# Gate and up projections of a decoder trunk: high and low halves of x as one 512-column operand

## The chip, the core and the metric

The kernel runs on one core of a Trainium2 chip. The metric is the device time of one execution in microseconds. Engines are called as the profile calls them: PE is TensorE's matmul, PEld its weight load, DVE is VectorE, ACT is ScalarE, POOL is GpSimd, SP is SyncE, which issues the DMAs.

## The reference

Four layers over 256 tokens of width 1024, all in float32. Each layer is a half-step SwiGLU, a token mixer and another half-step SwiGLU, each followed by a layer norm. The change touches the SwiGLU alone, which occurs eight times:

```python
D_MODEL = 1024; SEQ = 256; DEPTH = 4; D_FF = 2816

def swiglu(x, w13, w2):
    gate, up = jnp.split(x @ w13, 2, axis=-1)
    return (jax.nn.silu(gate) * up) @ w2

for i in range(DEPTH):
    x = layer_norm(ALPHA * x + 0.5 * swiglu(x, ffn1_w13[i], ffn1_w2[i]), ln_g[i, 0], ln_b[i, 0])
    ...   # token mixer: sparse attention, forgetting attention, latent attention, sparse attention
    x = layer_norm(ALPHA * x + 0.5 * swiglu(x, ffn2_w13[i], ffn2_w2[i]), ln_g[i, 2], ln_b[i, 2])
```

## The kernel before

**Three products for one.** Every float32 matrix product is made of three TensorE products in float32r. Each operand is split into a high half (the value rounded to float32r, an ACT cast) and a low half (the value minus the high half, a DVE subtraction), and high·high, high·low and low·high are added up in one PSUM bank. `mm3` and `mm3b` (lines 154 and 160) issue the three for one K tile of 128.

**Operands.** x is kept transposed: `xh` and `xl` (`new_xt`, line 191) hold its high and low halves, 8 K tiles by 256 tokens each. `transpose_x` fills them through PSUM. Weights come by `unit` (line 126): SP loads 512 KB into one of 6 `raw` buffers, ACT casts it into the first half of a `slot` (line 141), DVE subtracts into the second half (line 142). There are 15 slots, shared with other operands; a slot is given back when the products that read it are done. A product's stationary operand is 128 columns wide, its moving operand 256 or 512.

**The SwiGLU** (`ffn`, line 280) has 22 column tiles of 128 in gate and in up. In seven of the eight the first four tiles are made with x as the stationary operand (`proj`); the change leaves that. The rest goes by pairs of column tiles: 11 pairs in the first SwiGLU, 9 in the others, 74 in all. A pair has two parts, gate (part 0) and up (part 1), so there are 148 parts. A part has two units of four K tiles each, and `projb` (line 180) is called for column tile i = 0 and i = 1: for each of 8 K tiles `mm3b` issues high weight with `xh`, low weight with `xh`, high weight with `xl`, each with 256 moving columns into one half of a bank. That is 48 products in a part. The two column tiles share one bank of the tag `psa` (4 banks): `pg` for gate, `pu` for up. The attention mixer of layer 2 calls `projb` too, for 128 products of each line; the change leaves those.

After the gate part ACT takes Silu of the whole bank in one instruction (line 338; in the very first pair two, line 336); after the up part DVE multiplies by the up bank (line 341), and `split` (lines 187 and 188) makes the two halves of the result, `ht`. Behind each pair come 24 products of 512 columns of the second matmul, `out_mm` (line 256, through `mm3`, lines 156 to 158, tag `psb`), for a pair of tiles finished earlier. After the last pair `out_end` runs the tiles that are left, pair 8 first, then 9, then 10; 18 products stand ahead of the first one that reads the last pair's `ht`. A layer norm follows.

**Order.** The tile framework sets the order of each engine's instructions when the kernel is built, and each engine runs its own in that order. The order rows below name the profile's tiles with their buffer numbers.

Of the kernel before, what the change touches and what calls it, by code (L numbers as in the profile page):

```python
# [17 lines left out]
F32R = mybir.dt.float32r  # L18
AF = mybir.ActivationFunctionType
# [3 lines left out]
P = 128  # L23
D = 1024
SEQ = 256
NT = SEQ // P
DEPTH = 4
KT = D // P
# [22 lines left out]
class Net:  # L51
# [128 lines left out]
    def projb(self, us, i, out, k0=0):  # L180

        c = slice(i * P, (i + 1) * P)
        for k, (h, l) in enumerate(us, k0):
            self.mm3b(out, h[:, c], l[:, c], self.xh[:, k, :], self.xl[:, k, :], k == 0, k == KT - 1)

    def split(self, hi, lo, src):
        self.nc.scalar.copy(hi, src)  # L187
        self.nc.vector.tensor_sub(lo, src, hi.bitcast(F32))  # L188


    def new_xt(self):
        self.xh = self.t(self.sp, [P, KT, SEQ], F32R, "xh", 1)
        self.xl = self.t(self.sp, [P, KT, SEQ], F32R, "xl", 1)

    def transpose_x(self, t, h):
        ps = self.ps("b")
# [83 lines left out]
    def ffn(self, w13, w2, ln, first=False, last=False):  # L280
        nc = self.nc
        ht = {}
        self.begin_out(w2, NFF // 2, lambda i: ht[i], "b")
        f0, turns = 0, []
        if not first:

            f0 = 4
            z = self.slot(2, 4, SEQ)
            gh, gl = z[:, 0], z[:, 1]
            for i in range(4):  # L290
                ht[i] = (gh[:, i], gl[:, i])
            gate, up = self.cols(w13, 0, 512), self.cols(w13, DFF, 512)
            for t in range(NT):
                pg, pu = self.ps(), self.ps()
                self.proj(gate, t, pg)
                s = self.tok()
                nc.scalar.activation(s, pg, AF.Silu)
                if t:
                    turns.pop()()
                self.proj(up, t, pu, KT // 2)  # L300
                nc.vector.tensor_mul(s, s, pu)

                def turn(t=t, s=s):
                    pt = self.ps("b")
                    for i in range(4):
                        nc.tensor.transpose(pt[:, i * P:(i + 1) * P], s[:, i * P:(i + 1) * P], self.ident)
                    c = (slice(None), slice(None), slice(t * P, (t + 1) * P))
                    self.split(gh[c], gl[c], pt.rearrange("p (k c) -> p k c", k=4))

                turns.append(turn)  # L310
        pairs = (NFF - f0) // 2
        self.pieces = 1
        for j in range(pairs):
            f = f0 + 2 * j
            if j % 2 == 0:
                zz = self.slot(2, 2, 2, SEQ)
            cold = first and not f
            pg, pu = self.ps(), self.ps()

            p2 = self.ps()[:, SEQ:] if cold else pg[:, SEQ:]  # L320
            s = self.tok()
            for part, p in enumerate(((pg[:, :SEQ], p2), (pu[:, :SEQ], pu[:, SEQ:]))):
                c0 = part * DFF + f * P
                cut = KT // 2 if cold and not part else KT
                for k0 in range(0, KT, cut):
                    us = self.unit(self.rows(w13, k0, k0 + cut, c0, c0 + 2 * P))
                    if cut < KT and not k0:
                        self.load_x(1)
                    if k0:
                        for t in range(NT):  # L330
                            self.transpose_x(t, 1)
                    for i in range(2):
                        self.projb(us, i, p[i], k0)
                if part == 0 and cold:
                    for i in range(2):
                        nc.scalar.activation(s[:, i * SEQ:(i + 1) * SEQ], p[i], AF.Silu)
                elif part == 0:
                    nc.scalar.activation(s, pg, AF.Silu)
                    if turns:
                        turns.pop()()  # L340
            nc.vector.tensor_mul(s, s, pu)
            z = zz[:, j % 2]
            self.split(z[:, 0], z[:, 1], s.rearrange("p (i c) -> p i c", i=2))
            for i in range(2):
                ht[f + i] = (z[:, 0, i], z[:, 1, i])
            if j == 5:
                self.load_ln(*ln)
            if first and j == 2:
                self.late_consts()
            k = j - 2 + f0 // 2  # L350
            if 0 <= k < 8:
                for t in range(NT):
                    self.out_mm(k, t)
            if j == pairs - 1:
                for k in range(k + 1, 8):
                    for t in range(NT):
                        self.out_mm(k, t)
        for t in range(NT):
            self.out_end(t, (8, 9, 10))
            self.layer_norm(t, self.acc[t], 2.0 * ALPHA, 4.0 * LN_EPS, last)  # L360
# [535 lines left out]
```

## Time and profile before

| | us |
|---|---|
| median of 3 runs | 2048.35 (2045.14 to 2049.26) |
| the profiled execution | 2049.12 |
| its span, first to last instruction | 2047.4 |
| PE busy | 2017.6 (99%) |
| PEld busy | 1855.6 (91%) |
| DVE busy | 1261.7 (62%) |
| ACT busy | 1017.9 (50%) |
| POOL busy | 140.1 (7%) |
| mean granted share of TensorE's clock | 0.993 |

PE's products are pipelined: a product's bar in the trace is longer than the distance to the next one's start, so what a product costs in a dense run is read from starts, not from its mean duration. The profiled execution is 1.7 us longer than its span and 0.8 us over the median of the runs.

### The profile page before, as it was taken

The numbers are of one execution on the slowest core, as the hardware profiler recorded it, in microseconds if no ns is written. First come the engines' busy times: TensorE is split into PE (matmuls) and PEld (weight loads), VectorE is DVE, ScalarE is ACT, GpSimd is POOL, SyncE is SP. The second block draws the span as 40 slices with busy tenths as digits, with TensorE's granted clock in tenths as the row PEclk, the third lists the DMA queues.
The fourth block names the chain that finished last, engine by engine and source line by source line (L and its number), as shares of the span: only waits on it lengthen the run. The fifth ranks groups of instructions, "written<-read, shape, count | busy, mean of one in ns | idle before, by whom it ended". The sixth has DMA issues, their size and how long they took to land.

```text
span 2047.4 us, 33890 instructions
## 1 busy us (share of the span) xinstructions
PE 2017.6 (99%) x13430; PEld 1855.6 (91%) x13430; DVE 1261.7 (62%) x2064; ACT 1017.9 (50%) x1579; POOL 140.1 (7%) x324
## 2 busy tenths in 40 slices
PE   9999999999999999999999999999999999999998
PEld 8998998999899988799989998789989999988997
DVE  6444799545654469954564456964465455997453
ACT  6443476444444347644454436854444444675441
POOL 0000310000000022000000003000000003200000
PEclk9999999999999999999999999999999999999999
DMA  9754546656655454665665542575556554447550
GB/s 310 223 186 122 164 131 189 208 186 186 206 185 186 146 184 136 206 199 187 190 197 186 188 124 94 155 240 186 188 175 212 186 172 152 130 144 240 185 186 22
DMA packets 253023, 362.98 MB, mean 177 GB/s; under 512 B 11856, under 2 KB 204128, under 8 KB 252864
## 3 DMA queue, kind: packets, MB, share of 16 engines
q1 hardware_dynamic: 252080, 358.30, 55.7%
q0 software_dynamic: 784, 2.51, 0.4%
q8 instruction: 106, 1.74, 0.4%
q14 instruction: 53, 0.43, 0.1%
HBM read 359.69 MB, written 1.06 MB: 176 GB/s over the span
## 4 chain that ended last, share of the span: by engine, by line
PE 92%; DVE 3%; ACT 2%; DMA 2%; issue 1%; POOL 0%; SPq 0%; DVEq 0%; ACTq 0%; POOLq 0%
PE psa L163 14%; PE psa L164 14%; PE psa L162 14%; PE psb L156 8%; PE psb L157 8%; PE psb L158 8%; PE psa L156 7%; PE psa L157 7%; PE psa L158 7%; DMA raw<-in_ffn_w 1%; PE psb L199 1%; ACT slot L141 1%; ACT s L400 1%; DVE slot L142 1%; PE psb L162 0%
## 5 line engine op out<-in xcount | busy, mean ns | idle before, releaser
L142 DVE TENSOR_TENSOR slot<-raw,slot 128x1024 fp32r<-128x1024 f32 (+4 forms) x719 | 795.5, 1126 | 622.7 <-ACT slot L141 618.8
L141 ACT CAST slot<-raw 128x1024 fp32r<-128x1024 f32 (+4 forms) x719 | 680.6, 972 | 671.0 <-issue 344.3
L163 PE MATMUL psa<-xh,slot 128*128 128x256 f32 x2496 | 707.7, 284 | 0.2 <-DVE slot L142 0.2
L162 PE MATMUL psa<-xh,slot 128*128 128x256 f32 x2496 | 707.8, 284 | 0.0
L164 PE MATMUL psa<-xl,slot 128*128 128x256 f32 x2496 | 707.5, 283 | 0.0
L163 PEld LDWEIGHTS psa<-xh,slot 128*128 128x128 f32 x2496 | 480.2, 192 | 3.4 <-DVE slot L142 0.4
L162 PEld LDWEIGHTS psa<-xh,slot 128*128 128x128 f32 x2496 | 479.9, 192 | 3.1
L164 PEld LDWEIGHTS psa<-xl,slot 128*128 128x128 f32 x2496 | 480.2, 192 | 0.0
L156 PE MATMUL psb<-slot,slot 128*128 128x512 f32 (+2 forms) x800 | 306.8, 384 | 0.0
L157 PE MATMUL psb<-slot,slot 128*128 128x512 f32 (+2 forms) x800 | 306.0, 383 | 0.0
L158 PE MATMUL psb<-slot,slot 128*128 128x512 f32 (+2 forms) x800 | 304.5, 381 | 0.0
L156 PE MATMUL psa<-slot,xh 128*128 128x256 f32 (+5 forms) x736 | 242.9, 330 | 3.2 <-ACT xh L187 3.2
L157 PE MATMUL psa<-slot,xh 128*128 128x256 f32 (+5 forms) x736 | 239.7, 326 | 0.0
L158 PE MATMUL psa<-slot,xl 128*128 128x256 f32 (+5 forms) x736 | 238.4, 325 | 0.0
L158 PEld LDWEIGHTS psb<-slot,slot 128*128 128x128 f32 (+1 forms) x800 | 150.3, 188 | 29.3
L156 PEld LDWEIGHTS psb<-slot,slot 128*128 128x128 f32 (+1 forms) x800 | 150.5, 188 | 27.8 <-ACT slot L187 0.9
L157 PEld LDWEIGHTS psb<-slot,slot 128*128 128x128 f32 (+1 forms) x800 | 150.7, 188 | 26.1 <-DVE slot L188 0.7
L156 PEld LDWEIGHTS psa<-slot,xh 128*128 128x128 f32 x736 | 141.5, 192 | 14.2 <-ACT xh L187 4.1
L157 PEld LDWEIGHTS psa<-slot,xh 128*128 128x128 f32 x736 | 141.4, 192 | 10.2
L158 PEld LDWEIGHTS psa<-slot,xl 128*128 128x128 f32 x736 | 140.8, 191 | 10.6
L77 POOL MEMSET slot<- 128x1 f32 (+1 forms) x88 | 8.7, 101 | 1395.1 <-PE psb L158 1031.8
L187 ACT CAST slot<-psb 64x256 fp32r<-64x256 f32 (+4 forms) x158 | 63.4, 411 | 39.4 <-DVE slot L188 25.9
(149 smaller groups left out, 1600.2 us busy)
## 6 DMA issues: line engine op xcount, KB each, us to landing
raw<-in_ffn_w SPq DMA_DIRECT2D x528, 512.0 KB, 4.2
raw<-in_dsa_w_in SPq DMA_DIRECT2D x48, 512.0 KB, 4.4
raw<-in_w_out SPq DMA_DIRECT2D x32, 512.0 KB, 3.6
raw<-in_fox_w_in SPq DMA_DIRECT2D x24, 512.0 KB, 3.9
ln_g<-in_ln_g SPq DMA_DIRECT2D x12, 512.0 KB, 5.3
ln_b<-in_ln_b SPq DMA_DIRECT2D x12, 512.0 KB, 6.3
slot<-scratch_cum POOLq DMA_DIRECT2D x4, 512.0 KB, 6.4
raw<-in_mla_w_ukv SPq DMA_DIRECT2D x4, 512.0 KB, 4.0
```

The source lines that it names most:

```text
L77: self.nc.gpsimd.memset(z[:, :1] if dt == F32 else z[:, :1].bitcast(F32), 0.0)
L141: nc.scalar.copy(h[:, c], raw[:, c])
L142: nc.vector.tensor_sub(l[:, c], raw[:, c], h[:, c].bitcast(F32))
L156: mm(out, sh, mh, start=start, stop=False)
L157: mm(out, sh, ml, start=False, stop=False)
L158: mm(out, sl, mh, start=False, stop=stop)
L162: mm(out, sh, mh, start=start, stop=False)
L163: mm(out, sl, mh, start=False, stop=False)
L164: mm(out, sh, ml, start=False, stop=stop)
L187: self.nc.scalar.copy(hi, src)
L199: self.nc.tensor.transpose(ps[:, i * P:(i + 1) * P], self.x[t][:, k * P:(k + 1) * P], self.ident)
L400: nc.scalar.activation(sv, sv, AF.Exp, bias=nb[:, c:c + 1], scale=scale, accum_out=l[:, c:c + 1])
```

## The change

`xh` and `xl` become two halves of one tile `xx`, so that for a K tile the 256 high and the 256 low columns of x lie side by side. A new `projw` takes the place of `projb` in the pairs of the SwiGLU: for four K tiles at a time it issues, for both column tiles, the high weight with all 512 columns of `xx`, and then, for both column tiles, the low weight with the 256 high columns, added to the second half of the bank. A column tile now takes a whole bank. A new `joined` adds the two halves of a bank on the way out: ACT copies the second half into SBUF, DVE adds the first half to it. Silu reads the sum from SBUF, one instruction for each column tile; the multiplication reads both factors from SBUF.

```diff
+    def projw(self, us, outs, k0=0):
+        mm = self.nc.tensor.matmul
+        for g in range(0, len(us), 4):
+            four = list(enumerate(us[g:g + 4], k0 + g))
+            for i, out in enumerate(outs):
+                for k, (h, _) in four:
+                    mm(out, h[:, i * P:(i + 1) * P], self.xx[:, k], start=k == 0, stop=False)
+            for i, out in enumerate(outs):
+                for k, (_, l) in four:
+                    mm(out[:, 1], l[:, i * P:(i + 1) * P], self.xh[:, k], start=False, stop=k == KT - 1)
+
+    def joined(self, dst, ps):
+        self.nc.scalar.copy(dst, ps[:, 1])
+        self.nc.vector.tensor_add(dst, ps[:, 0], dst)
...
-        self.xh = self.t(self.sp, [P, KT, SEQ], F32R, "xh", 1)
-        self.xl = self.t(self.sp, [P, KT, SEQ], F32R, "xl", 1)
+        self.xx = self.t(self.sp, [P, KT, 2, SEQ], F32R, "xx", 1)
+        self.xh, self.xl = self.xx[:, :, 0], self.xx[:, :, 1]
...
-            pg, pu = self.ps(), self.ps()
-            p2 = self.ps()[:, SEQ:] if cold else pg[:, SEQ:]
-            s = self.tok()
-            for part, p in enumerate(((pg[:, :SEQ], p2), (pu[:, :SEQ], pu[:, SEQ:]))):
+            s, u = self.tok(), self.tok()
+            for part, d in enumerate((s, u)):
...
+                pw = [self.ps().rearrange("p (a c) -> p a c", a=2) for _ in range(2)]
...
-                    for i in range(2):
-                        self.projb(us, i, p[i], k0)
-                if part == 0 and cold:
-                    for i in range(2):
-                        nc.scalar.activation(s[:, i * SEQ:(i + 1) * SEQ], p[i], AF.Silu)
-                elif part == 0:
-                    nc.scalar.activation(s, pg, AF.Silu)
-                    if turns:
-                        turns.pop()()
-            nc.vector.tensor_mul(s, s, pu)
+                    self.projw(us, pw, k0)
+                for i in range(2):
+                    di = d[:, i * SEQ:(i + 1) * SEQ]
+                    self.joined(di, pw[i])
+                    if part == 0:
+                        nc.scalar.activation(di, di, AF.Silu)
+                if part == 0 and turns:
+                    turns.pop()()
+            nc.vector.tensor_mul(s, s, u)
```

In the changed file `projw` issues at lines 195 (512 columns) and 198 (256), `joined` at 202 (ACT) and 203 (DVE), `split` at 206 and 207, Silu stands at 354 and the multiplication at 357.

PE in the gate part of the fourth pair of the first SwiGLU, before: the last K tile of column tile 0 and the first of column tile 1 (`psa_55_540` is the bank, the two slots are its two weight units).

```order
L162 MATMUL psa_55_540<-xh_5_86,slot_61_549 128x256
L163 MATMUL psa_55_540<-xh_5_86,slot_61_549 128x256
L164 MATMUL psa_55_540<-xl_6_87,slot_61_549 128x256
L162 MATMUL psa_55_540<-xh_5_86,slot_59_544 128x256
L163 MATMUL psa_55_540<-xh_5_86,slot_59_544 128x256
L164 MATMUL psa_55_540<-xl_6_87,slot_59_544 128x256
```

The same part now, whole:

```order
L195 MATMUL psa_64_479<-xx_5_86,slot_67_482 128x512 x4
L195 MATMUL psa_65_480<-xx_5_86,slot_67_482 128x512 x4
L198 MATMUL psa_64_479<-xx_5_86,slot_67_482 128x256 x4
L198 MATMUL psa_65_480<-xx_5_86,slot_67_482 128x256 x4
L195 MATMUL psa_64_479<-xx_5_86,slot_69_487 128x512 x4
L195 MATMUL psa_65_480<-xx_5_86,slot_69_487 128x512 x4
L198 MATMUL psa_64_479<-xx_5_86,slot_69_487 128x256 x4
L198 MATMUL psa_65_480<-xx_5_86,slot_69_487 128x256 x4
```

48 products of 256 columns have become 16 of 512 and 16 of 256, on two banks in place of one. Outside the parts PE's products, transposes and their order are the same.

ACT around the end of the same gate part, before: Silu of the whole bank stands between the casts of later weight units, and the last row is the cast of the result's high half.

```order
L141 CAST slot_90_860<-raw_89_859 128x1024
L338 ACTIVATE tok_57_542<-psa_55_540 128x512
L141 CAST slot_92_865<-raw_91_864 128x1024
L141 CAST slot_94_919<-raw_93_918 128x1024
L141 CAST slot_96_924<-raw_95_923 128x1024
L187 CAST slot_35_368<-tok_57_542 128x512
```

The same stretch now:

```order
L141 CAST slot_104_758<-raw_103_757 128x1024
L202 COPY tok_62_477<-psa_64_479 128x256
L202 COPY tok_62_477<-psa_65_480 128x256
L141 CAST slot_106_763<-raw_105_762 128x1024
L354 ACTIVATE tok_62_477<-tok_62_477 128x256 x2
L141 CAST slot_110_808<-raw_109_807 128x1024
L202 COPY tok_63_478<-psa_70_529 128x256
L202 COPY tok_63_478<-psa_71_530 128x256
L141 CAST slot_112_813<-raw_111_812 128x1024
L206 CAST slot_39_325<-tok_62_477 128x512
```

Two copies stand at the end of each part, and the Silu behind them is two instructions with a weight cast ahead of it.

DVE at the end of the first SwiGLU, before: the last weight unit's subtraction, the multiplication, the low half of the last pair's result, the layer norm's first step.

```order
L142 TENSOR_TENSOR slot_216_1950<-raw_215_1949,slot_216_1950 128x528
L341 TENSOR_TENSOR tok_168_1653<-tok_168_1653,psa_167_1652 128x512
L188 TENSOR_TENSOR slot_165_1649<-tok_168_1653,slot_165_1649 128x512
L229 SCALAR_TENSOR_TENSOR x0_1_71,lnst_191_1842<-x0_1_71,psb_51_512 128x512
```

And now:

```order
L142 TENSOR_TENSOR slot_246_1726<-raw_245_1725,slot_246_1726 128x528
L203 TENSOR_TENSOR tok_195_1449<-psa_202_1500,tok_195_1449 128x256
L203 TENSOR_TENSOR tok_195_1449<-psa_203_1501,tok_195_1449 128x256
L357 TENSOR_TENSOR tok_194_1448<-tok_194_1448,tok_195_1449 128x512
L207 TENSOR_TENSOR slot_193_1446<-tok_194_1448,slot_193_1446 128x512
L248 SCALAR_TENSOR_TENSOR x0_1_71,lnst_221_1618<-x0_1_71,psb_58_449 128x512
```

Two additions have come between the last product of the up part and the multiplication.

## Rows read from the trace of the kernel before

**Rows 1.** The page: busy time of the engines, and TensorE's granted clock by slices.

```profile
PE 2017.6 (99%) x13430; PEld 1855.6 (91%) x13430; DVE 1261.7 (62%) x2064; ACT 1017.9 (50%) x1579; POOL 140.1 (7%) x324
PEclk9999999999999999999999999999999999999999
```

**Rows 2.** The page: the chain that ended last, by engine and by line.

```profile
PE 92%; DVE 3%; ACT 2%; DMA 2%; issue 1%; POOL 0%; SPq 0%; DVEq 0%; ACTq 0%; POOLq 0%
PE psa L163 14%; PE psa L164 14%; PE psa L162 14%; PE psb L156 8%; PE psb L157 8%; PE psb L158 8%; PE psa L156 7%; PE psa L157 7%; PE psa L158 7%; DMA raw<-in_ffn_w 1%; PE psb L199 1%; ACT slot L141 1%; ACT s L400 1%; DVE slot L142 1%; PE psb L162 0%
```

**Rows 3.** Groups by line and shape: xcount | busy us, mean ns | idle before.

```profile
L162 PE MATMUL psa<-xh,slot 128*128 128x256 f32 x2496 | 707.8, 284 | 0.0
L163 PE MATMUL psa<-xh,slot 128*128 128x256 f32 x2496 | 707.7, 284 | 0.2 <-DVE slot L142 0.2
L164 PE MATMUL psa<-xl,slot 128*128 128x256 f32 x2496 | 707.5, 283 | 0.0
```

**Rows 4.** Timeline of PE over one pair: start us, bar us, line, operands.

```profile
402.24 0.28 PE L162 MATMUL psa<-xh,slot 128*128 128x256 f32 x1
...
413.76 0.40 PE L156 MATMUL psb<-slot,slot 128*128 128x512 f32 x1
...
419.22 0.28 PE L162 MATMUL psa<-xh,slot 128*128 128x256 f32 x1
```

**Rows 5.** Stretches: us, busy us of each engine, granted clock, DMA share, GB/s.

```profile
402.24:419.22 16.98, 16.98 (x121) 16.02 (x120) 8.37 (x8) 7.30 (x9) 0.10 (x1) 1.00 0.60 187
201.30:208.10 6.80, 6.09 (x24) 5.98 (x24) 6.80 (x10) 4.09 (x6) 2.56 (x4) 0.50 0.49 163
771.30:778.10 6.80, 4.24 (x19) 4.05 (x20) 6.53 (x19) 6.73 (x20) 1.85 (x3) 0.50 0.01 4
1331.10:1337.90 6.80, 4.73 (x14) 3.46 (x13) 6.28 (x12) 4.48 (x7) 0.99 (x1) 0.50 0.55 161
```

**Rows 6.** Timeline of PE at the end of the first SwiGLU's last pair.

```profile
181.76 0.28 PE L164 MATMUL psa<-xl,slot 128*128 128x256 f32 x1
181.88 0.40 PE L156 MATMUL psb<-slot,slot 128*128 128x512 f32 x1
...
183.27 0.39 PE L156 MATMUL psb<-slot,slot 128*128 128x512 f32 x1
183.50 0.39 PE L157 MATMUL psb<-slot,slot 128*128 128x512 f32 x1
...
185.99 0.39 PE L156 MATMUL psb<-slot,slot 128*128 128x512 f32 x1
```

**Rows 7.** Groups by line and shape of ACT and DVE.

```profile
L779 ACT COPY tok<-psa 128x256 f32<-128x256 f32 x8 | 3.0, 380 | 3.5 <-PE psa L158 3.5
L336 ACT ACTIVATE tok<-psa 128x256 f32<-128x256 f32 x2 | 0.8, 385 | 1.4 <-PE psa L164 1.4
L400 ACT ACTIVATE s<-s,nb 128x256 f32<-128x256 f32 x64 | 31.9, 501 | 0.0
L338 ACT ACTIVATE tok<-psa 128x512 f32<-128x512 f32 x73 | 43.7, 598 | 37.2 <-PE psa L164 37.2
L188 DVE TENSOR_TENSOR slot<-psa,slot 128x256 fp32r<-128x256 f32 x32 | 13.5, 421 | 8.0 <-ACT slot L187 7.5
L142 DVE TENSOR_TENSOR slot<-raw,slot 128x1024 fp32r<-128x1024 f32 x580 | 699.7, 1222 | 574.0 <-ACT slot L141 570.3
L141 ACT CAST slot<-raw 128x1024 fp32r<-128x1024 f32 x580 | 597.1, 1049 | 607.5 <-issue 313.0 <-PE psb L158 146.4 <-PE psa L164 99.3
```

**Rows 8.** Timelines of ACT and DVE at the place of rows 6.

```profile
182.08 0.69 DVE L341 TENSOR_TENSOR tok<-tok,psa 128x512 f32<-128x512 f32 x1
182.86 0.62 ACT L187 CAST slot<-tok 128x512 fp32r<-128x512 f32 x1 [1.54 <-DVE tok L341]
183.51 0.69 DVE L188 TENSOR_TENSOR slot<-tok,slot 128x512 fp32r<-128x512 f32 x1 [0.74 <-ACT slot L187]
```

**Rows 9.** Timeline of all engines at the start: first products of the first pair.

```profile
8.87 0.51 PE L162 MATMUL psa<-xh,slot 128*128 128x256 f32 x2
10.13 0.58 PE L163 MATMUL psa<-xh,slot 128*128 128x256 f32 x1 [0.20 <-DVE slot L142]
```

## The prediction

> **What bounds the kernel now.** I read the page first: PE is busy for 99% of the span and its clock is at full level in nearly every slice [rows 1]. A busy PE alone proves little, since its bars overlap, so the chain that ended last comes next: 92% of it is PE, and the three lines of `mm3b`, 162 to 164, are 14% each [rows 2]. PE's own products set the end, and what counts is how far apart they start. The groups give the number of products: 2496 on each of the three lines, with almost no idle time ahead of them [rows 3]. 128 of each belong to the attention mixer, so the parts have 2496 − 128 = 2368 on each line, which is 148 parts of 16.
>
> The distance between starts is read from one pair in the middle of a SwiGLU, at a granted clock of 1.00 [rows 5], whose first row is this pair. From 402.24 to 413.76 PE issues the pair's 96 products of 256 columns: 11.52 us, 120.0 ns each. From 413.76 to 419.22 it issues 24 of 512 columns: 5.46 us, 227.5 ns each [rows 4]. So 256 more columns cost 107.5 ns, and 120.0 − 107.5 = 12.5 ns of each product do not depend on its columns. That fixed share is what the change can save: PE's columns stay the same, the number of products falls.
>
> **The change part by part.**
>
> Products. A part had 48 products of 256 columns: 48 × 0.1200 = 5.76 us. It now has 16 of 512 and 16 of 256: 16 × 0.2275 + 16 × 0.1200 = 5.56 us. The part gets 0.20 us shorter, and 148 parts give **29.6 us**. The same from the other side: 2368 pairs of products become one product each, and each saves 12.5 ns. All of it lies on the path that sets the end, since PE is the chain there [rows 2].
>
> The price of a 512-column product is the number that matters, and the trace has it from `out_mm`, with another moving operand. At the end of the first SwiGLU both ends are to be seen: from 181.88 to 183.27 six products take 1.39 us, 231.7 ns each, and from 183.50 to 185.99 eleven take 2.49 us, 226.4 ns each [rows 6]. With 226.4 the change saves 2368 × 13.6 = 32.2 us, with 231.7 it saves 2368 × 8.3 = 19.7 us. I take 227.5, the mean over a whole block between parts, with ACT, DVE and the DMAs at work beside it as they will be in a part.
>
> The Trainium skill has another price. Its page "TensorE: Matmul & The Clock Gate", section "Back-to-back issue gap", puts the isolated distance of N columns at full clock at N/2.4 + 2.5 ns, an estimate of 109.2 ns for 256 columns and 215.8 for 512, so that joining two would save 2.5 ns, 5.9 us in all. The trace disagrees, with 120.0 and 227.5 [rows 4], and the measurement decides; the rule comes back as a rival below.
>
> Work on the way out of PSUM. Each part adds two ACT copies of 128x256 from PSUM and two DVE additions. An ACT copy of that shape takes 380 ns; the nearest DVE instruction, one operand in PSUM, takes 421 ns. Silu was one of 598 ns and is now two, each between 385 and 501 ns [rows 7], 0.17 to 0.40 us more. For a pair ACT goes from 7.30 us [rows 5] to 7.30 + 4 × 0.380 + 0.40 = 9.2 us at most, DVE from 8.37 to 8.37 + 4 × 0.421 = 10.05 us. The pair itself becomes 11.12 + 5.46 = 16.58 us, so ACT is busy for 55% and DVE for 61% of it. This work costs nothing as long as it hides beside PE; without that cover it would be about 1.6 us of each engine for each pair.
>
> A new wait. A column tile has a bank of its own now, so the four banks hold one pair in place of two. A part's first products wait for DVE's addition that frees the bank of the same part one pair earlier. Before, a bank was needed again two pairs later, so it had the other part, the 24 products and a whole pair, 5.76 + 5.46 + 16.98 = 28 us. Now it has the other part and the 24 products, 5.56 + 5.46 = 11.0 us, and in the first pairs of the first SwiGLU, which have no such 24, 5.56 us. Emptying takes two copies and an addition, 0.76 + 0.42 = 1.2 us; with a weight cast (1049 ns) and a weight subtraction (1222 ns) [rows 7] queued ahead it takes 3.5 us. I cost it at nothing. Behind ACT's waiting copies weight casts are queued, but their slots are filled well ahead of use, and a unit's slot is given back after half a part now, before it after three quarters (first unit) or all of it.
>
> The end of each SwiGLU. The last pair's result is needed 18 products after its last part. Before, those run from 181.88 to 185.99 [rows 6], and the subtraction that makes the result is done at 183.51 + 0.69 = 184.20 [rows 8]: 1.8 us to spare. Now a copy and an addition, 0.80 us, come ahead of the multiplication, and 1.0 us is left. A weight subtraction of 1.22 us in the way would make it 0.2 us late, eight times: 0 to 2 us. I take 0.
>
> The start. PE's second and third products stand 1.26 us apart at most while DVE makes the first low weights [rows 9]; with eight high products ahead that wait goes. Against it the first product now needs the low half of x too, and the transposes of the second half of x stand behind 16 products. Between 1.3 us gained and 2.5 us lost (a weight unit, 1.05 + 1.22, in a row); I take 0.
>
> The clock. Three stretches of 6.8 us have a granted clock of 0.50 [rows 5]: the half level, 1.2 GHz. All lie at or in the mixers, where PE had waited. The change moves them in time, not their cause; one that goes or comes is worth at most 3.4 us. I take 0, and two of them, 6.8 us, as the low bound, one as the high.
>
> Sum: 2049.12 − 29.6 = 2019.5 us for the profiled execution, which lies 0.8 us over the median: **2018.7 us**.
>
> **The rivals.**
>
> The wide product saves nothing or next to nothing. If a product that reads both halves of `xx` costs what two of 256 columns cost, 240.0 ns, the time stays at 2048. For it speaks only that no row shows this operand as a 512-column one; against it that no stretch of rows 4 and 6 has a 512-column product above 231.7 ns. By the page's rule above it would end at 2042.
>
> Part of the gain is eaten. If parts wait 0.1 us each on the average for weights or banks, half the gain is left: 2048.35 − 14.8 = 2034 us. For it: ACT and DVE get 1.7 to 1.9 us more work for each pair, in an order fixed beforehand. Against it: both stay idle for over a third of the pair.
>
> Slower. The bank is free too late: DVE's addition stands behind a weight subtraction that itself waits for its slot, and the part starts late. If every up part waits one subtraction, 74 × 1.22 = 90 us come to the 29.6 saved: 2109 us. It decides from 24 late parts of 148 on (29.6 / 1.22). For it: the time to empty a bank falls from 28 to 11 us, and the copies wait on PE in the queue that also feeds it. Against it: 11.0 us stand against 3.5, so some six more weight instructions would have to be in the way. The Trainium skill speaks against the change here: the same page, section "A second HAM failure mode: psum-queue depth-cycling", tells of 512-column products whose cycling through PSUM banks left PE idle so often that its clock went between the two levels. In the stretch of rows 5, whose 24 products already change banks, the clock is 1.00, which does not bear it out.
>
> **How the numbers follow.** The forecast has 0.80, the product that saves nothing 0.07 (0.04 within 0.2%, 0.03 faster at 2042), the half gain 0.06, slower 0.07. A measurement of this kernel can tell about 0.2%, 4 us, from no change. Faster is 0.80 + 0.03 + 0.06 = 0.89, same 0.04, slower 0.07. The range goes from 2048.35 − 32.2 − 6.8 = 2009 to 2048.35 − 19.7 + 3.4 + 2 + 2.5 = 2036 us; it takes in the half gain and leaves out the other two rivals, 0.14.
>
> **What would show it.** PE should have 13430 − 2368 = 11062 products, 2368 of them 512 columns wide at line 195, 227 ns apart, and a part should take 5.56 us, a pair about 16.6 us. The clock in the pairs should stay at 1.00. ACT should be busy for about 9 us of a pair, DVE for 10. No wait of a part's first product for the additions of line 203 should add up to more than 2 us over the run. Wide products 232 ns apart or more, or PE idle ahead of lines 195 or 198, would make the forecast wrong.

## The result and the profile after

The changed kernel takes 2020.24 us in the median (2019.7 to 2020.38), the kernel before 2048.24 (2045.14 to 2049.26): a ratio of 0.9867, with a 95% interval from 0.9856 to 0.9879. That is 28.0 us less; 29.6 were forecast, and the time lies inside the range. The profiled execution took 2020.33 us, 28.8 less than the one of before.

The page of the changed kernel, busy time, clock and chain, as in [rows 1, 2]:

```profile
PE 1989.1 (99%) x11062; PEld 1730.7 (86%) x11062; DVE 1391.8 (69%) x2360; ACT 1123.4 (56%) x1948; POOL 140.8 (7%) x324
PEclk9999999999999999999999999999999999999999
PE 93%; DVE 3%; ACT 2%; issue 1%; DMA 1%; POOL 0%; SPq 0%; DVEq 0%; ACTq 0%
PE psa L195 27%; PE psa L198 14%; PE psb L156 9%; PE psb L157 9%; PE psb L158 8%; PE psa L156 7%; PE psa L157 7%; PE psa L158 7%; PE psb L218 1%; ACT slot L141 1%; DVE slot L142 1%; ACT s L416 1%; PE psb L162 1%; PE psa L162 0%; PE psa L164 0%
```

PE has 11062 products, 2368 fewer, and its own products still make the chain. DVE and ACT have 130 and 105 us more to do. The page looks as full as before, which shows again that a busy PE tells nothing of what a product costs.

Groups by line and shape of the changed kernel, the new instructions (count | busy us, mean ns | idle before):

```profile
L195 PE MATMUL psa<-xx,slot 128*128 128x512 f32 x2368 | 593.5, 393 | 1.7 <-ACT slot L141 1.7
L198 PE MATMUL psa<-xx,slot 128*128 128x256 f32 x2368 | 330.3, 282 | 0.0
L203 DVE TENSOR_TENSOR tok<-psa,tok 128x256 f32<-128x256 f32 x296 | 125.5, 425 | 82.5 <-ACT tok L202 74.7
L202 ACT COPY tok<-psa 128x256 f32<-128x256 f32 x296 | 110.0, 372 | 207.5 <-PE psa L198 192.2
L354 ACT ACTIVATE tok<-tok 128x256 f32<-128x256 f32 x148 | 53.9, 412 | 1.4 <-DVE tok L203 1.1
```

The prices taken from [rows 7] held: 372 ns for the copy (380), 425 for the addition (421), 412 for Silu (385 to 501).

The timeline of PE over the pair that answers to [rows 4]; equal products that follow each other are one row, so a row's start and the next row's start are eight products apart:

```profile
397.48 1.98 PE L195 MATMUL psa<-xx,slot 128*128 128x512 f32 x8
399.30 1.11 PE L198 MATMUL psa<-xx,slot 128*128 128x256 f32 x8
400.25 2.00 PE L195 MATMUL psa<-xx,slot 128*128 128x512 f32 x8
402.09 1.11 PE L198 MATMUL psa<-xx,slot 128*128 128x256 f32 x8
403.04 2.00 PE L195 MATMUL psa<-xx,slot 128*128 128x512 f32 x8
404.88 1.12 PE L198 MATMUL psa<-xx,slot 128*128 128x256 f32 x8
...
408.63 0.40 PE L156 MATMUL psb<-slot,slot 128*128 128x512 f32 x1
...
414.10 1.98 PE L195 MATMUL psa<-xx,slot 128*128 128x512 f32 x8
```

The two parts take 408.63 − 397.48 = 11.15 us (11.12 forecast, 11.52 before), the pair 16.62 (16.58 forecast, 16.98 before). A look at the groups: the first eight wide products, which come behind the wide ones of the second matmul, take 1.82 us by these rounded rows, some 227 ns each. The later groups, behind narrow products, take 1.84 us, 230 ns each. Eight narrow ones take 0.95 us, 119 ns each.

The stretches that answer to [rows 5]: the same pair, and those at the low clock outside the start and the end of the run (the second and third row lie inside stretches of 3.41 us):

```profile
397.48:414.10 16.62, 16.62 (x90) 14.34 (x88) 10.16 (x12) 8.75 (x14) 0.10 (x1) 1.00 0.63 189
199.80:203.10 3.30, 3.30 (x14) 3.30 (x14) 3.30 (x6) 2.71 (x3) 1.17 (x3) 0.50 0.60 173
763.00:766.30 3.30, 3.30 (x17) 3.30 (x17) 3.17 (x8) 3.25 (x6) 0.00 (x0) 0.50 0.00 0
1309.10:1319.30 10.20, 6.85 (x20) 5.41 (x21) 9.44 (x17) 6.22 (x9) 1.39 (x2) 0.50 0.56 174
```

In the pair the clock stays at 1.00, DVE is busy for 10.16 us and ACT for 8.75.

Where the 28.8 us went is read from the first and the last product of the parts of each SwiGLU. For the second SwiGLU, in the kernel before:

```profile
367.86 0.28 PE L162 MATMUL psa<-xh,slot 128*128 128x256 f32 x1
...
515.52 0.28 PE L164 MATMUL psa<-xl,slot 128*128 128x256 f32 x1
```

and in the changed one, with the first product behind the parts:

```profile
363.81 1.98 PE L195 MATMUL psa<-xx,slot 128*128 128x512 f32 x8
...
507.36 1.12 PE L198 MATMUL psa<-xx,slot 128*128 128x256 f32 x8
508.31 0.40 PE L156 MATMUL psb<-slot,slot 128*128 128x512 f32 x1
```

147.66 us have become 508.31 − 0.12 − 363.81 = 144.38 (the last narrow product starts 0.12 us ahead of the next): 3.28 us for 18 parts, 0.18 us each. All seven later SwiGLUs show the same 3.28 us to 0.01, together 23.0. The first one goes from 172.90 to 170.45 us, 2.45 less, and begins 0.44 us earlier. The sparse-attention mixer of the first layer takes 1.16 us less and the forgetting-attention mixer 1.90 us less, though nothing in them was changed. The remaining mixers are 0.07 us longer each. The sum is 28.8.

### The profile page after: what moved, and what is told of

The parts are those of the page before. It is cut to its first block, busy times and chain, and to the rows that moved or that the text cites. A ratio compares the mean times of both kernels' runs of the same rounds, so it can differ in the third digit from the quotient of the medians.

```text
span 2018.6 us, 29613 instructions
## 1 busy us (share of the span) xinstructions
PE 1989.1 (99%) x11062; PEld 1730.7 (86%) x11062; DVE 1391.8 (69%) x2360; ACT 1123.4 (56%) x1948; POOL 140.8 (7%) x324
## 4 chain that ended last, share of the span: by engine, by line
PE 93%; DVE 3%; ACT 2%; issue 1%; DMA 1%; POOL 0%; SPq 0%; DVEq 0%; ACTq 0%
PE psa L195 27%; PE psa L198 14%; PE psb L156 9%; PE psb L157 9%; PE psb L158 8%; PE psa L156 7%; PE psa L157 7%; PE psa L158 7%; PE psb L218 1%; ACT slot L141 1%; DVE slot L142 1%; ACT s L416 1%; PE psb L162 1%; PE psa L162 0%; PE psa L164 0%
## 5 line engine op out<-in xcount | busy, mean ns | idle before, releaser
L195 PE MATMUL psa<-xx,slot 128*128 128x512 f32 x2368 | 593.5, 393 | 1.7 <-ACT slot L141 1.7
L195 PEld LDWEIGHTS psa<-xx,slot 128*128 128x128 f32 x2368 | 431.4, 189 | 82.0 <-ACT slot L141 1.9
L198 PEld LDWEIGHTS psa<-xx,slot 128*128 128x128 f32 x2368 | 323.3, 191 | 23.1
L198 PE MATMUL psa<-xx,slot 128*128 128x256 f32 x2368 | 330.3, 282 | 0.0
L156 PE MATMUL psa<-slot,xx 128*128 128x256 f32 (+5 forms) x736 | 242.5, 329 | 3.1 <-ACT xx L206 3.1
L157 PE MATMUL psa<-slot,xx 128*128 128x256 f32 (+5 forms) x736 | 239.4, 325 | 0.0
L158 PE MATMUL psa<-slot,xx 128*128 128x256 f32 (+5 forms) x736 | 238.6, 325 | 0.0
L202 ACT COPY tok<-psa 128x256 f32<-128x256 f32 x296 | 110.0, 372 | 207.5 <-PE psa L198 192.2
L203 DVE TENSOR_TENSOR tok<-psa,tok 128x256 f32<-128x256 f32 x296 | 125.5, 425 | 82.5 <-ACT tok L202 74.7
L156 PEld LDWEIGHTS psa<-slot,xx 128*128 128x128 f32 x736 | 141.2, 192 | 14.1 <-ACT xx L206 3.9
L158 PEld LDWEIGHTS psa<-slot,xx 128*128 128x128 f32 x736 | 140.6, 191 | 10.6
L157 PEld LDWEIGHTS psa<-slot,xx 128*128 128x128 f32 x736 | 141.0, 192 | 10.2
```

The source lines that it names most:

```text
L156: mm(out, sh, mh, start=start, stop=False)
L157: mm(out, sh, ml, start=False, stop=False)
L158: mm(out, sl, mh, start=False, stop=stop)
L195: mm(out, h[:, i * P:(i + 1) * P], self.xx[:, k], start=k == 0, stop=False)
L198: mm(out[:, 1], l[:, i * P:(i + 1) * P], self.xh[:, k], start=False, stop=k == KT - 1)
L202: self.nc.scalar.copy(dst, ps[:, 1])
```

## The experiments

All eight start from the changed kernel. Each differs in the few lines shown; e9 is the changed kernel itself. The length of a SwiGLU is read in each trace as above, from the first product of its parts to the last.

**e1: the same order, without the wide product.**

```diff
-                    mm(out, h[:, i * P:(i + 1) * P], self.xx[:, k], start=k == 0, stop=False)
+                    mm(out[:, 0], h[:, i * P:(i + 1) * P], self.xh[:, k], start=k == 0, stop=False)
+                    mm(out[:, 1], h[:, i * P:(i + 1) * P], self.xl[:, k], start=False, stop=False)
```

> The changed kernel with each wide product made as two of 256 columns again: high weight with the high half of xx into the first half of the bank, high weight with its low half into the second. Order of the groups, banks, copies and additions stay as in the changed kernel. Theory (each product has a fixed share of about 12.5 ns, and the gain is the 2368 products saved): a part takes 48 x 0.120 = 5.76 us in place of the 5.585 us measured, so 2020.2 + 148 x 0.175 = 2046 us. Rival (the gain comes from the new order, with high weights ahead of low ones, and from banks of their own): 2020 to 2025 us.

Measured: 2048.12 us (2045.53 to 2049.99), a ratio to the kernel before of 1.0001 (0.9991 to 1.0011). The whole gain is gone, with the order, the banks, the copies and the additions of the changed kernel still there. 2046 was expected from a part of 5.585 us; with the 11.15 / 2 = 5.575 us of the rows above the same sum gives 2047.6. Its pair in the timeline:

```profile
403.63 0.28 PE L195 MATMUL psa<-xx,slot 128*128 128x256 f32 x1
...
415.14 0.40 PE L156 MATMUL psb<-slot,slot 128*128 128x512 f32 x1
...
420.61 0.28 PE L195 MATMUL psa<-xx,slot 128*128 128x256 f32 x1
```

96 products in 11.51 us and a pair of 16.98 us are those of [rows 4]. Each of the seven later SwiGLUs takes 147.66 us, as in the kernel before. So there the gain is the number of products, and neither the new order nor the new banks have a share in it. The first SwiGLU is another matter: here it takes 174.43 us, against 172.90 in the kernel before, and the run also begins 1.0 us later. The profiled execution makes these 2.5 us up in the mixers, two of which have a stretch at the low clock of 3.4 us in place of 6.8. That the two totals agree so closely is therefore in part chance.

**e2: wide and narrow products in turn.**

```diff
             for i, out in enumerate(outs):
-                for k, (h, _) in four:
+                for k, (h, l) in four:
                     mm(out, h[:, i * P:(i + 1) * P], self.xx[:, k], start=k == 0, stop=False)
-            for i, out in enumerate(outs):
-                for k, (_, l) in four:
                     mm(out[:, 1], l[:, i * P:(i + 1) * P], self.xh[:, k], start=False, stop=k == KT - 1)
```

> The changed kernel with the groups of four undone: for each column tile and each K tile the wide product, and right behind it the narrow one of the low weight. As many products of each width as in the changed kernel. Theory of the fixed share alone: 2020 us, within 2 us, since only the number of products counts. Rival (the grouping is what helps): slower. Second theory, from the changed kernel's trace, in which the first five wide products behind narrow ones are 229 to 236 ns apart and later ones 226.5, and the first narrow one behind wide ones 114: if each switch has its own price at the first product alone, a wide and a narrow product take 233.5 + 114 = 347.5 ns, as much as now (348.4 on the average), so 2018 to 2020 us; if every product here is of the dearer kind, 233 + 120 = 353 ns, so 2020 + 2368 x 0.0046 = 2031 us.

Measured: 2030.88 us (2028.74 to 2034.46), ratio 0.9920 (0.9898 to 0.9941). The fixed share alone does not give this: with the same products of each width it is some 10 us slower than the changed kernel, and the 2031 us that were worked out for the dearer kind throughout are met. The timeline of PE, each product a row:

```profile
396.77 0.40 PE L192 MATMUL psa<-xx,slot 128*128 128x512 f32 x1
397.00 0.28 PE L193 MATMUL psa<-xx,slot 128*128 128x256 f32 x1
397.12 0.40 PE L192 MATMUL psa<-xx,slot 128*128 128x512 f32 x1
...
399.59 0.40 PE L192 MATMUL psa<-xx,slot 128*128 128x512 f32 x1
```

From 396.77 to 399.59 eight of each take 2.82 us, 352.5 ns for two; in groups of four, over the whole pair, two take 11.15 / 32 us, 348.4 ns. Each of the seven later SwiGLUs takes 145.82 to 145.85 us in place of 144.38, together 10.1 us of the 10.6 us between the two kernels. So without the grouping over a third of the 28 us would be lost, because wide products are dearer behind narrow ones.

**e3 and e8: groups of eight K tiles; e9: the changed kernel beside it.**

```diff
-        for g in range(0, len(us), 4):
-            four = list(enumerate(us[g:g + 4], k0 + g))
+        for g in range(0, len(us), 8):
+            four = list(enumerate(us[g:g + 8], k0 + g))
```

> The changed kernel with groups of eight K tiles in place of four: all wide products of a part, then all its narrow ones, so one change of width inside a part goes. Fixed share alone: 2020 us. With the second theory (the five wide products behind narrow ones take some 27 ns more together, the first narrow one behind wide ones 6 ns less): 21 ns less in each of 148 parts, 3.1 us, so 2017 us. Rival (grouping low weights later helps by taking waits away): no further gain, 2020 us, since no such waits are left in the trace.

> The kernel with groups of eight K tiles once more, beside the changed kernel on one chip. In the trace of its first run the 18 parts of a later SwiGLU took 144.02 us against 144.38 in the changed kernel, 20 ns less a part. Theory (one switch from narrow to wide products less in each part): 148 x 0.020 = 3.0 us less than the changed kernel measures here. Rival (chance of the runs): the same within 1 us.

> The changed kernel as it is, for the comparison with groups of eight on one chip: 2020 us, within 1.5 us, 28 us less than the kernel before.

Measured: 2018.87 us (2017.73 to 2019.66) for e3, ratio 0.9859 (0.9840 to 0.9878), where 2017 was expected. On another chip 2017.17 (2016.8 to 2017.8) for e8 against 2018.55 (2018.3 to 2020.75) for the changed kernel in e9: 1.4 us less, where 3.0 were expected. e9 is 28.2 us below the kernel before on that chip (2046.78). In the trace of e8 the gain is plain. PE over a pair:

```profile
395.50 3.79 PE L195 MATMUL psa<-xx,slot 128*128 128x512 f32 x16
399.12 2.08 PE L198 MATMUL psa<-xx,slot 128*128 128x256 f32 x16
401.04 3.82 PE L195 MATMUL psa<-xx,slot 128*128 128x512 f32 x16
...
412.07 1.29 PE L195 MATMUL psa<-xx,slot 128*128 128x512 f32 x5
```

The pair takes 16.57 us, 0.05 less than in groups of four, and each later SwiGLU 144.02 us in both runs, 0.36 less, 2.5 us over seven. As a whole the gain is smaller than what a measurement of this kernel can tell; still, all four runs of e8 lie below all four of e9.

**e4: three times the work on the way out.**

```diff
         self.nc.scalar.copy(dst, ps[:, 1])
+        for _ in range(2):
+            z = self.w([P, 256], "spare", 2)
+            self.nc.scalar.copy(z, ps[:, 1])
+            self.nc.vector.tensor_add(z, ps[:, 0], z)
         self.nc.vector.tensor_add(dst, ps[:, 0], dst)
```

> The changed kernel with the copy and the addition on the way out of PSUM made three times in place of once, the two more into a buffer that nobody reads. ACT gets 8 x 0.372 = 3.0 us more for a pair, DVE 8 x 0.425 = 3.4 us, and they are then busy for about 12 and 13.5 of 16.6 us. Theory (this work is hidden beside TensorE): 2020 to 2022 us. Rival (the work on the way out eats part of the gain, and is the 1.6 us that are missing from the forecast): twice that more, 2023.5 us or above; and if the cover breaks, 2030 us or more.

Measured: 2022.84 us (2021.07 to 2024.18), ratio 0.9878 (0.9859 to 0.9898). By the total it falls between the two expectations, and the trace decides. The stretch of the pair:

```profile
397.40:414.02 16.62, 16.62 (x90) 14.33 (x88) 12.83 (x21) 10.72 (x22) 0.10 (x1) 1.00 0.61 191
```

The pair takes 16.62 us, as in the changed kernel, with DVE busy for 12.83 us of it in place of 10.16. Each later SwiGLU takes 144.38 us, the same to the last digit. The work is hidden where it stands, even three times over. Of the 2.6 us that the profiled execution lost, 2.3 lie in the forgetting-attention mixer, where a stretch at the low clock was 6.8 us long in place of 3.4. Only this execution has a trace; that the other runs are slower for the same reason is not shown.

**e5: two banks for all parts.**

```diff
+        pw = [self.ps().rearrange("p (a c) -> p a c", a=2) for _ in range(2)]
         for j in range(pairs):
...
-                pw = [self.ps().rearrange("p (a c) -> p a c", a=2) for _ in range(2)]
```

> The changed kernel with two banks for all parts of a SwiGLU in place of a pair of the four in turn: a part can start only when the part just before it is out of PSUM. The order that is built puts 3 of the 24 products of the second matmul between gate and up, the other 21 behind the up part. Theory (the gain holds because the banks have 11 us to be emptied in the changed kernel): here an up part has 3 products, 0.68 us, and the 0.96 us by which column tile 0 is done earlier, against a copy and an addition, 0.80 us, plus whatever weight cast or subtraction (1.05, 1.22 us) stands ahead in the queues. So waits of up to 1.2 us for 74 up parts, 0 to 89 us; with 0.4 us on the average 2020 + 30 = 2050 us, and the waits stand in the trace ahead of the wide products, released by the additions. Rival (emptying a bank is quick enough that the number of banks plays no part): 2020 to 2023 us.

Measured: 2024.56 us (2022.14 to 2026.25), ratio 0.9887 (0.9869 to 0.9905): 6.0 us over the changed kernel on the same chip, not the 30 I expected. PE between gate and up in the middle of a SwiGLU, DVE's additions there, and PE's waits on the additions over the whole run (us, times, longest):

```profile
403.76 1.11 PE L198 MATMUL psa<-xx,slot 128*128 128x256 f32 x8
405.41 2.00 PE L195 MATMUL psa<-xx,slot 128*128 128x512 f32 x8
```

```profile
404.84 0.90 DVE L203 TENSOR_TENSOR tok<-psa,tok 128x256 f32<-128x256 f32 x2 [0.41 <-ACT tok L202]
```

```profile
PE psa L195 <- DVE tok L203: 1.5, 3, 0.7
```

From 403.76 to 405.41 are 1.65 us: eight narrow products, 0.95, and three of the second matmul, 0.70. No wait is left between them. The first column tile is out of PSUM by the time the second one's narrow products and those three are through, since no weight cast or subtraction stood in the way, but only just: of the two additions the first ends near 405.3. The three waits that there are lie in the first SwiGLU, which has no second matmul in its first pairs. They are 1.5 us of the 2.35 us by which the first SwiGLU is longer than in the changed kernel (172.80 against 170.45). The later ones have their parts 0.91 to 0.97 us longer, since three products of the second matmul have moved in between, and the stretch behind them, where no mixer follows, about 0.7 us shorter: some 0.3 us each. If that holds for all seven, it adds up to about 4 us; the rest of the 6.0 was not followed up.

**e7: wide products in four pieces.**

```diff
-                    mm(out, h[:, i * P:(i + 1) * P], self.xx[:, k], start=k == 0, stop=False)
+                    for q in range(4):
+                        c = slice((q % 2) * P, (q % 2 + 1) * P)
+                        mm(out[:, q // 2, c], h[:, i * P:(i + 1) * P], self.xx[:, k, q // 2, c],
+                           start=k == 0 and q == 0, stop=False)
```

> The changed kernel with each wide product made as four of 128 columns, in the same place, each with the same high weight: how far down the fixed share holds. If a product costs 12.5 ns and its columns, 128 of them cost 53.75 + 12.5 = 66 ns, four 265 ns against the 229.9 measured for a wide one: 2020 + 2368 x 0.035 = 2103 us. If below some width another limit takes over, as the transposes of 128 columns in the trace suggest, which start 108 to 110 ns apart, four take 436 ns: 2020 + 2368 x 0.206 = 2508 us.

Measured: 2540.0 us in one run. PE in a part:

```profile
499.84 3.69 PE L197 MATMUL psa<-xx,slot 128*128 128x128 f32 x32
503.36 1.17 PE L201 MATMUL psa<-xx,slot 128*128 128x256 f32 x8
504.37 3.69 PE L197 MATMUL psa<-xx,slot 128*128 128x128 f32 x32
```

2508 was expected for another limit and 2103 for the fixed share. 32 pieces take 3.52 us, 110.0 ns each on the average, where columns and fixed share would make 66. The narrow products behind them take 1.01 us by eight, 126 ns each on the average. Each piece loads its weights anew, 9472 loads on that line. So the fixed share is no law for every width: at 128 columns another limit has taken over.

## Why the prediction was right, point by point

- **What bounds the kernel.** Right: with 2368 products fewer, and nothing else that would shorten PE's work, the time fell, and e1 took it back by putting the products back, to 147.66 us in each of the seven later SwiGLUs.
- **The price of the products.** The mechanism was right, its size 10% too large. The forecast had 227.5 ns for every wide product. That was a mean over two prices. The block of 24 in [rows 4] stands behind narrow products too, and its sixth product in the kernel before is

```profile
414.92 0.39 PE L158 MATMUL psb<-slot,slot 128*128 128x512 f32 x1
```

  The first five take 414.92 − 413.76 = 1.16 us, 232 ns each, the other nineteen 4.30 us, 226.3. In the changed kernel three of a pair's four groups follow narrow products, and with only eight products in a group the five dear ones weigh more: 230 ns. The narrow ones gave a little back, 119 for 120. A part saved 0.18 us, not 0.20, and the parts of the seven later SwiGLUs 23.0 us, not 25.2. The dearer price stood in [rows 6] as well, six products at 231.7 ns behind narrow ones and then 226.4; I read it as a spread and not as an order.
- **The way out of PSUM.** Right: ACT 8.75 us a pair (at most 9.2), DVE 10.16 (10.05), hidden, and in e4 still hidden with three times the copies and additions.
- **The new wait.** Right. PE's waits of the changed kernel have none on the additions; the only one ahead of the new products is at the start:

```profile
PE psa L195 <- ACT slot L141: 1.7, 1, 1.7
```

  e5 shows that the slower rival was further off than the forecast put it: even with half the banks the bank is free in time, but for three waits of 1.5 us in all.
- **The end of a SwiGLU.** Right. In the first one DVE's last instruction ahead of the layer norm, and PE's first product that reads it:

```profile
181.51 0.69 DVE L207 TENSOR_TENSOR slot<-tok,slot 128x512 fp32r<-128x512 f32 x1 [0.76 <-ACT slot L206]
```

```profile
183.10 0.39 PE L156 MATMUL psb<-slot,slot 128*128 128x512 f32 x1
```

  181.51 + 0.69 = 182.20, so 0.9 us are to spare; 1.0 was worked out.
- **The start.** Taken as 0, it cost about 1.5 us. PE at the start of the changed kernel, and a stretch of it as above, with a granted clock of 0.50:

```profile
8.43 3.62 PE L195 MATMUL psa<-xx,slot 128*128 128x512 f32 x8
11.85 1.18 PE L198 MATMUL psa<-xx,slot 128*128 128x256 f32 x8
...
15.24 2.11 PE L195 MATMUL psa<-xx,slot 128*128 128x512 f32 x8 [1.67 <-ACT slot L141]
```

```profile
8.60:12.00 3.40, 3.40 (x10) 2.66 (x9) 1.49 (x2) 1.05 (x1) 0.00 (x0) 0.50 1.10 360
```

  Both things named for it came. The wait for the first low weights went, and the second weight unit is late by 1.67 us behind 16 products, eight of them at 3.42 / 8 = 428 ns under the low clock. The 22 parts of the first SwiGLU saved 2.45 us where 22 × 0.18 = 4.0 would be due. It also began 0.44 earlier, but that is chance: in e9, the same kernel, it begins at 8.96 us, later than the 8.87 of [rows 9].
- **The clock.** Taken as 0, it gave about 3 us back. The stretches at the low clock that begin near 200 and 763 us last 3.4 us each; those of before at 201 and 771 lasted 6.8 [rows 5]. The two mixers around them are shorter by 1.16 and 1.90 us. The third has grown to 10.2 us, and its mixer is only 0.07 us longer. At the second and third place this is luck of the moment: the second is 6.8 us again in e4, and the third is 6.8 in e9, the same kernel. At the first, no trace of the changed kernel or of an experiment has more than 3.4 us, so there the cause is open. Without these 3 us the profiled execution would lie some 4 us over its forecast of 2019.5, in place of 0.8. The medians hold a gift of the clock too. On the chip of e9, runs with the same mean clock are 24 to 26 us apart (0.996: 2018.30 to 2018.59 against 2044.31; 0.995: 2020.75 against 2044.40 and 2045.11). That is near the 23.0 + 2.45 us that the parts saved in the traces. So of the 28.0 us the products gave, by this reckoning, some 25, and the forecast of 29.6 came as near as it did with help from a term that it had put at nothing.
- **The product that saves nothing.** The rule of the Trainium skill, page "TensorE: Matmul & The Clock Gate", section "Back-to-back issue gap", gives by the prediction's estimate 5.9 us. It is not borne out for these products: 28.0 were measured, and 230 and 119 ns between starts stand against the estimates of 215.8 and 109.2 that follow from it.

## What to carry to other kernels

Where TensorE's own products are the chain, read the distance between their starts at two widths. The part that does not grow with the columns is paid for each product, and joining two products that share a stationary operand saved it once here, at 256 and 512 columns; in pieces of 128 another limit ruled. Put products of one width together, since here each change from narrow to wide cost time too. The work that this moved to other engines was free here; whether it is can be read from the stretch in question, and not from the page's average.

## What the runs showed of the hardware

- **A fixed share of a float32r product.** At a granted clock of 1.00 products of 256 columns start 120.0 ns apart [rows 4], and products of 512 columns 226.3, when they follow each other in a long run (sixteen in 3.62 us in e8; eleven at 226.4 in [rows 6]). So 256 columns cost 106.3 ns, and 13 to 14 ns of each product do not depend on the columns; the 12.5 of the prediction come from a block with the dearer products below in it. Every product here has a weight load of its own, 11062 of each on the page, and e1 put both back together. Whether the share belongs to the product or to its load no run tells. At 128 columns the distance is 110.0 ns on the average (e7). The Trainium skill, page "TensorE: Matmul & The Clock Gate", section "LDWEIGHTS (loading the stationary operand)", puts a weight load at P/1.2 ns for P columns, an estimate of 106.7 ns for 128. The 110.0 ns are near it, as they would be if the load set the pace of the pieces; no run here shows the load by itself.
- **Wide products are dearer behind narrow ones.** In the changed kernel eight of them take 1.84 us behind narrow ones, where eight of a long run take 1.81 (at 226.3 ns). In the second matmul of the kernel before the first five take 232 ns each and the rest 226.3. A wide and a narrow one take 352.5 ns when they alternate (e2) against 348.4 in groups. In e8, with one change less in each part, a pair is 0.05 us shorter. What makes the first wide products late was not found.
